# A decoder layer's expert stage: sums, norm and output unit by unit, in place of a last pass

## The chip, the cores and the metric

One core of one Trainium2 chip runs the whole kernel. The metric is device time of one launch in microseconds (us), lower is better; the median of three runs stands for the kernel.

## The reference

One decoder layer on x of 1024 tokens by 1024 (f32): a token mixer, a cross-attention, then the part that matters here, a mixture of experts with a residual and a layer norm. `h` is the second norm's output, `alpha = 2 ** 0.25`.

```python
h = layer_norm(alpha * h + memory_cross_attention(...), ln_x_g, ln_x_b)
p_g = softmax(h @ w_rg + b_rg); g = argmax(p_g)                     # one of 4 groups
e_val, e_idx = top_k((h @ w_re[g] + b_re[g]), 2)                    # two of its 8 experts
gate = p_g[g] * softmax(e_val)
y = sum(gate[c] * (silu(h @ w_gate[e]) * (h @ w_up[e])) @ w_down[e] for c, e in enumerate(e_idx))
out = layer_norm(alpha * h + y, ln_ffn_g, ln_ffn_b)
```

So each token has two experts, of one group, and 2048 (token, expert) rows are to be computed. An expert's weights are 12 tiles of 512 KB (8 for gate and up, 4 for down); 32 experts have 384.

## The kernel before

Up to about 840 us of the span come the mixer, the cross-attention, its norm and the router, tile by tile (8 tiles of 128 tokens). In the last loop over tiles (`for t in range(NT)`, L1101) PE's order is written out by hand; the other engines' order comes from a scheduler. `norm_pre`, `norm_stats` and `norm_post` make h2 (written to `h2_d` in DRAM), `route_a` finds the experts, `gates_` the gates, `route_b` each row's place within its expert; these run one tile behind the products of the next tile. Loads of the experts' weights into `ring` tiles are issued in this loop from SP: 35 tiles, and 42 with those added at L1190 and L1191.

After the loop, PE's and DVE's order is by hand (L1129). The last tile is normed and routed, then the lists are made. A **unit** is 32 rows of one expert; an expert has as many units as it needs, at least one, and the router's choice decides how many there are in all (78 here). `ohu` and `ohr` are one-hot matrices; their 16 f32 products (L1166) put, for each of 96 units and 32 places, the number of the row into `pi_`; from it come `gidx` (which quarter rows of h2 to gather) and `yidx` (where to write the result in `y_d`).

Then the experts' stage (`tile_critical`, L1368) runs with one program for each engine and semaphores by hand. A unit lies as 128 partitions x 256: 4 quarters of a row by 32 rows.

- SP loads weights into the ring, in the order in which experts run (expert 0 of each group, then expert 1 of each, ...). A load waits until the last unit of the expert that used its slot has done its `up` or `down` product.
- POOL gathers each unit's rows of h2 by an indirect DMA into `xg` (`get`, 8 ahead) and writes results by another (`put`).
- PE does `up` (64 products) and `down` (32 products). An expert's first `up` comes first, then for each further unit `up`, `down`, and then the last `down`.
- DVE turns `xg` (`rows`), multiplies by silu's result, turns again for `down`. ACT does silu and copies `down`'s result out of PSUM into `ys` (L1287).

Then comes the last pass (L1374 to L1395): for each tile, h2 and both results of each token are loaded, added with the gates, normed and written to `out`.

## Time and profile before

| | us |
|---|---|
| median of 3 runs | 1468.98 (1468.28 to 1471.16) |
| the profiled execution's own time | 1469.68 |
| its span, first to last instruction | 1467.9 |
| PE busy in the span | 1269.6 (86%) |
| DVE busy | 646.6 (44%) |
| ACT busy | 384.4 (26%) |
| POOL busy | 263.2 (18%) |

The span is what the rows below divide up; the profiled execution took 1.8 us more than its span. Busy times overlap between engines, so they don't add up to it.

### The profile page before, as it was taken

What the parts mean: (1) busy time and instruction counts of PE and PEld (TensorE: products, weight loads), DVE (VectorE), ACT (ScalarE), POOL (GpSimd) and SP (SyncE); (2) the same over time, 40 slices, a digit from 0 to 9 for tenths busy, and PEclk for the clock granted to TensorE, in tenths of its full rate; (3) what the DMA queues carried; (4) which work ended last, traced back from release to release, by engine and by line L of the source; (5) the groups of instructions that cost most, each with busy time, mean ns of one, the idle gap of its engine ahead of it and who ended that gap; (6) DMA issues with size and microseconds to landing.
All of it is one profiled execution on the core that took longest, in us unless ns stands there. A gap on an engine that the chain in (4) does not pass through costs nothing.

```text
span 1467.9 us, 29380 instructions
## 1 busy us (share of the span) xinstructions
PE 1269.6 (86%) x12171; PEld 979.3 (67%) x12171; DVE 646.6 (44%) x1585; ACT 384.4 (26%) x897; POOL 263.2 (18%) x301
## 2 busy tenths in 40 slices
PE   7999989999999999999999948988989869888700
PEld 6788866666677888888888737766657625647500
DVE  6676465555666558236577741111111111111148
ACT  4344354454664114225321101110101000001000
POOL 1111000000000221000011123333233322323303
PEclk9999999999999999999999959999999997999955
DMA  7003110101347322213632678999999999999583
GB/s 232 1 8 101 45 44 26 55 22 40 107 128 280 115 72 87 58 36 99 231 126 102 221 278 318 386 387 405 406 406 405 404 407 407 403 407 403 199 349 138
DMA packets 87789, 306.15 MB, mean 209 GB/s; under 512 B 12968, under 2 KB 13192, under 8 KB 87664
## 3 DMA queue, kind: packets, MB, share of 16 engines
q1 hardware_dynamic: 71424, 259.03, 46.5%
q0 software_dynamic: 13504, 35.43, 6.9%
q10 hardware_dynamic: 2736, 9.96, 1.7%
q8 instruction: 86, 1.41, 0.4%
q14 instruction: 39, 0.32, 0.1%
HBM read 282.04 MB, written 27.03 MB: 211 GB/s over the span
## 4 chain that ended last, share of the span: by engine, by line
PE 72%; SPq 8%; DMA 7%; DVE 7%; issue 3%; ACT 2%; POOLq 0%; POOL 0%; ACTq 0%; DVEq 0%
PE pg L1255 14%; SPq L1366 8%; PE py__7925 L1265 7%; DMA ring<-in_wx_dram 5%; PE py L101 4%; PE py L102 4%; PE py L103 4%; PE avf L641 3%; PE S L599 2%; PE ptf L627 2%; PE Sx L101 2%; PE Sx L103 2%; PE Sx L102 2%; PE S L598 2%; PE pk L101 2%
## 5 line engine op out<-in xcount | busy, mean ns | idle before, releaser
L1255 PE MATMUL pg<-ring,mo 128*32 128x256 f32 x4992 | 310.3, 392 | 45.8 <-DVE mo L1307 24.6
L1255 PEld LDWEIGHTS pg<-ring,mo 128*32 128x32 f32 x4992 | 209.0, 112 | 134.8 <-DVE mo L1307 39.5
L1307 DVE STREAM_TRANSPOSE mo<-xg 128x256 f32<-128x256 f32 x79 | 35.2, 445 | 382.8 <-PE pg L1255 374.3
L1265 PE MATMUL py__7925<-ring,mo 128*32 128x256 f32 x2496 | 160.0, 385 | 38.4 <-DVE mo L1316 22.0
L1265 PEld LDWEIGHTS py__7925<-ring,mo 128*32 128x32 f32 x2496 | 108.9, 110 | 76.7 <-DVE mo L1316 32.9
L1327 POOL DMA_INDIRECT xg<-h_d,gidx x86 | 87.8, 1021 | 300.2 <-ACT ys L1287 178.0
L1293 ACT ACTIVATE mo<-pg 128x128 f32<-128x128 f32 x78 | 21.7, 278 | 390.1 <-PE pg L1255 390.1
L1334 POOL DMA_INDIRECT y_d<-ys,yidx x78 | 79.1, 1015 | 80.5 <-ACT ys L1287 65.3
L604 DVE CUSTOM_DVE_ANT_0 S<-S,cB 128x128 f32<-128x128 f32 (+7 forms) x64 | 49.0, 765 | 62.2 <-PE S L602 59.8
L1316 DVE STREAM_TRANSPOSE mo<-mo 128x128 f32<-128x128 f32 x78 | 24.3, 311 | 67.4 <-PE py__7925 L1265 64.1
L101 PE MATMUL py<-B,Pxh 128*128 128x512 f32 x128 | 53.3, 416 | 0.0
L608 ACT ACTIVATE Pf<-S,fm 128x128 f32<-128x128 f32 (+7 forms) x64 | 47.3, 740 | 20.3 <-DVE fl L614 11.9
L1287 ACT ACTIVATE ys<-py__7925 128x256 f32<-128x256 f32 x78 | 29.8, 382 | 85.0 <-PE py__7925 L1265 82.1
L103 PE MATMUL py<-B,Pxl 128*128 128x512 f32 x128 | 50.2, 393 | 0.0
L101 PE MATMUL py<-woh,oh 128*128 128x512 f32 x128 | 50.1, 392 | 0.0
L102 PE MATMUL py<-B,Pxh 128*128 128x512 f32 x128 | 50.1, 392 | 0.0
L102 PE MATMUL py<-wol,oh 128*128 128x512 f32 x128 | 50.0, 391 | 0.0
L103 PE MATMUL py<-woh,ol 128*128 128x512 f32 x128 | 50.0, 391 | 0.0
L103 PE MATMUL Sx<-Ah,h1l 128*128 128x512 f32 x128 | 49.8, 389 | 0.0
L101 PE MATMUL Sx<-Ah,h1h 128*128 128x512 f32 x128 | 49.8, 389 | 0.0
L102 PE MATMUL Sx<-Al,h1h 128*128 128x512 f32 x128 | 49.8, 389 | 0.0
L627 PE MATMUL ptf<-identF,Pf 128*128 128x128 f32 x288 | 43.2, 276 | 2.4 <-DVE Pf L615 2.4
(502 smaller groups left out, 2684.5 us busy)
## 6 DMA issues: line engine op xcount, KB each, us to landing
ring<-in_wx_dram SPq DMA_DIRECT2D x384, 512.0 KB, 7.8
yb<-y_d SPq DMA_DIRECT2D x16, 512.0 KB, 8.8
h_d<-h POOLq DMA_DIRECT2D x15, 512.0 KB, 3.0
wqkr<-in_wqk_dram SPq DMA_DIRECT2D x8, 512.0 KB, 3.7
cB<-c_d POOLq DMA_DIRECT2D x8, 512.0 KB, 4.1
wkr<-in_wxkv_dram SPq DMA_DIRECT2D x8, 512.0 KB, 4.8
wor<-in_w_out_dram SPq DMA_DIRECT2D x8, 512.0 KB, 3.7
wxqr<-in_wxqT_dram SPq DMA_DIRECT2D x8, 512.0 KB, 3.7
```

The costliest lines, as they stand in the source:

```text
L101: mm(o, ah, bh, start=st, stop=False, skip_group_check=True)
L102: mm(o, ah, bl, start=False, stop=False, skip_group_check=True)
L103: mm(o, al, bh, start=False, stop=sp, skip_group_check=True)
L604: nc.vector.tensor_tensor_reduce(S[:, 0:n], S[:, 0:n], CB[h][:, 0:n], scale=1.0, scalar=3.0e38, op0=OP.add, op1=OP.min, accum_out=m_)
L608: nc.scalar.activation(p_[:, 0:n], S[:, 0:n], AF.Exp, bias=m_, scale=-1.0, accum_out=l_)
L627: nc.tensor.transpose(pt[:, j], p_[:, (4 * a + j) * P:(4 * a + j + 1) * P], identF)
L641: mm(av[64 * h:64 * h + 64, q0:256], V[p // 2, j // 4][:, j % 4, c0:c0 + 64], PT[i2, h, j // 4][:, j % 4, q0:256], start=j == 0, stop=j == ...
L1255: i_ = mm(pg[32 * h:32 * h + 32], xT_[:, k], w_[:, :, h * P:h * P + P], start=k == 0, stop=k == ND - 1, skip_group_check=True)
L1265: i_ = mm(py_[32 * h:32 * h + 32], aT[:, c], w_[:, h * 256:h * 256 + 256], start=c == 0, stop=c == 3, skip_group_check=True)
L1327: e.indirect_dma_start(out=xg[v % NG], out_offset=None, in_=h2v, in_offset=bass.IndirectOffsetOnAxis(ap=gidx[:, v:v + 1], axis=0), bounds_ ...
L1334: e.indirect_dma_start(out=yv, out_offset=bass.IndirectOffsetOnAxis(ap=yidx[:, j:j + 1], axis=0), in_=ys[j % NY], in_offset=None, bounds_c ...
L1366: e.dma_start(ring[n % NRING], wx[ordr[s], k]).then_inc(s_w[n % NRING], 16)
```

## The change

In the experts' stage a unit's result is no longer written away to be summed later. Experts run in rising order within a group, so the lower-numbered expert of a token runs first. For a row of a token's **first** expert, the unit holds gate * result + h2 (h2 is what `xg` still holds), and this sum is written, unnormed, to the token's row of `out`. For a row of the **second** expert, `xg` is gathered a second time, now from `out` (`again`: rows of first experts have an index out of bounds and are left as they are); gate * result is added to it, the norm is applied, and the row of `out` is written again.

The norm needs sums over a row's four quarters, which lie on four partitions: `bn_stats` of each quarter goes into `qst`, a product with `same` on PE (`moments`) brings the four together, `bn_aggr` merges them; the power runs on POOL (`root`). `sec` and `fst` (1 or 0 for each row of a unit) choose between the normed and the plain sum. A unit's `moments` comes two `up`s after its own `up`, and its `down` now comes after the next `up`, over the border between experts too. `put` of a unit comes two steps behind; `again` of a unit waits for the landing of the write four units earlier. `y_d`, `yidx`, `ys` and the last pass are gone; `out` is filled with zeros once, in the router's loop.

The lists are made from bf16 one-hots: `ohA` holds 256 (t + 1) at a row's place, `ohB` (made on ACT) the rest of its number in units of that, so that two bf16 products give the whole number; 32 products in place of 16 f32 ones, and the 16 `ohu` instructions become two `eq`. Further products (`pgt`, `pgc`) bring the gates to the units' rows, as three bf16 parts. After the last loop the routing of the last tile comes ahead of the second half of its norm, its gates come last, and the first gather is issued ahead of the stage. One tile less is added to the ring (41).

In the router's loop and the lists:

```diff
-    ohr = [s4("ohr", (P, 4, 2, P)) for _ in range(2)]
+    ohA, ohB = s4("ohA", (P, NT, 2, P), BF16), s4("ohB", (P, NT, 2, P), BF16)
+    ohG = s4("ohG", (P, NT, 2, 96), BF16)
+    z_ = s4("z_")
+    nc.gpsimd.memset(z_, 0.0)
+    for t in range(NT):
+        nc.gpsimd.dma_start(out[t * P:t * P + P, :], z_)
...
-        nc.vector.tensor_tensor(ohr[t // 4][:, t % 4], io4[:, None, :].to_broadcast([P, 2, P]),
-                                rf[:, :, None].to_broadcast([P, 2, P]), op=OP.is_equal)
+        for c in range(2):
+            nc.vector.tensor_scalar(ohA[:, t, c], io4, rf[:, c:c + 1], 2.0 * P * (t + 1),
+                                    op0=OP.is_equal, op1=OP.mult)
+        for c in range(2):
+            nc.scalar.activation(ohB[:, t, c], ohA[:, t, c], AF.Copy, scale=lo[:, c:c + 1])
...
-    norm_post(NT - 1)
+    norm_mid(NT - 1)
     route_a(NT - 1, logits(NT - 1))
-    route_b(NT - 1)
-    gates_(NT - 1)
+    pr = ranks(NT - 1)
...
+    norm_post(NT - 1, mid=False)
...
-            nc.vector.tensor_scalar(ohu, io96, unit[:, t, c:c + 1], dst1[:, t, c:c + 1],
-                                    op0=OP.is_equal, op1=OP.mult)
-            mm(pi_, ohr[t // 4][:, t % 4, c], ohu, start=t + c == 0, stop=t + c == NT)
+    for h in (slice(0, NT), slice(NT, 2 * NT)):
+        nc.vector.tensor_tensor(eq[:, h], io96[:, None, :].to_broadcast([P, NT, 96]),
+                                unit.rearrange("p t (c o) -> p (t c) o", o=1)[:, h].to_broadcast([P, NT, 96]),
+                                op=OP.is_equal)
+        for n in range(h.start, h.stop):
+            for o_ in (ohA, ohB):
+                mm(pi_, o_[:, n // 2, n % 2], eq[:, n], start=n == 0 and o_ is ohA, stop=n == 2 * NT - 1 and o_ is ohB)
...
+    EARLY = 1
+    for v in range(EARLY):
+        gather(xg[v], h2v, gidx[:, v:v + 1])
...
+    for v_, src in ((g3q, g3), (b3q, b3)):
+        for q in range(4):
+            nc.gpsimd.dma_start(v_[32 * q:32 * q + 32], bass.AP(tensor=src.tensor, offset=src.offset + 256 * q,
+                                                                ap=[[0, 32], [1, 256]]))
...
+    gates_(NT - 1)
+    gate_rows(NT - 1)
...
-    ring_tiles(SLOTS - 4 - PRE[-1], s4p, "s4", load=False)
+    ring_tiles(SLOTS - 5 - PRE[-1], s4p, "s4", load=False)
```

`gate_rows`, new and also called for each tile in the loop, is nine small DVE instructions (three bf16 parts of the gates, and their product with a one-hot of the place). PE's and ACT's programs in the experts' stage:

```diff
+        def moments():
+            e.wait_ge(s_ms, r)
+            mm(pst.rearrange("p q n -> p (q n)"), same, qst.rearrange("p q n -> p (q n)"),
+               start=True, stop=True).then_inc(s_st, 1)
...
             up(s)
+            if s:
+                moments()
+                down(s - 1)
...
                     up(s)
+                    moments()
                     down(s)
...
-            down(s)
+        moments()
+        down(NEXP - 1)
+        e.reg_add(r, r, 1)
+        moments()
...
-            e.activation(ys[j % NY], py_, AF.Copy).then_inc(s_ev, 1)
+            e.activation(w1, vs[j % NV], AF.Copy, scale=fst[:, j:j + 1]).then_inc(s_w1, 1)
```

DVE's (its waits are left out; `total(j)` waits for `down` of unit j, for the second gather of j and for the landing of the write of unit j - 4):

```diff
+        def total(j):
...
+            e.scalar_tensor_tensor(v, py_, gcol[:, j:j + 1], xg[j % NG], op0=OP.mult, op1=OP.add).then_inc(s_ev, 1)
...
+            e.bn_stats(st, v).then_inc(s_bn, 1)
...
+            e.tensor_tensor(qst, st[:, None, :].to_broadcast([P, 4, 6]),
+                            qm[:, :, None].to_broadcast([P, 4, 6]), op=OP.mult).then_inc(s_ms, 1)
+        def norm_a(j):
...
+            e.bn_aggr(mv, pst.rearrange("p q n -> p (q n)")).then_inc(s_ag, 1)
...
+            e.scalar_tensor_tensor(w1, b3q, sec[:, j:j + 1], w1, op0=OP.mult, op1=OP.add).then_inc(s_w2, 1)
...
+            e.tensor_scalar(rs[:, 0:1], mv[:, 1:2], EPS / ALPHA ** 2, None, op0=OP.add).then_inc(s_r1, 1)
+            e.scalar_tensor_tensor(v, v, mv[:, 0:1], g3q, op0=OP.subtract, op1=OP.mult).then_inc(s_nm, 1)
+        def norm_b(j):
...
+            e.tensor_tensor(rs[:, 1:2], rs[:, 1:2], sec[:, j:j + 1], op=OP.mult).then_inc(s_r3, 1)
...
+            e.scalar_tensor_tensor(v, v, rs[:, 1:2], w1, op0=OP.mult, op1=OP.add).then_inc(s_o, 1)
         def step(i):
             if i + 1 < UMAX:
                 rows(i + 1)
             w8(e, s_si, i + 1)
             e.tensor_mul(a_[i % 2], a_[i % 2], pg[:, 1]).then_inc(s_mu, 1)
+            if i > 1:
+                norm_a(i - 2)
             w8(e, s_mu, B_MU + i + 1)
             w8(e, s_dn, i)
             e.transpose(mo[:, 512:640], a_[i % 2]).then_inc(s_at, 1)
+            if i > 1:
+                norm_b(i - 2)
+            if i:
+                total(i - 1)
```

and POOL's (`LA` is 6):

```diff
+        def again(v):
+            if v < UMAX:
+                w8(e, s_xt, v + 1)
+                if v > 3:
+                    w8(e, s_y[(v - 4) % NV], 16 * ((v - 4) // NV + 1))
+                gather(xg[v % NG], outv, aidx[:, v:v + 1]).then_inc(s_g[v % NG], 16)
...
         def step(i):
-            get(i + NG)
-            if i:
-                put(i - 1)
+            if i > 1:
+                root(i - 2)
+            get(i + LA)
+            if i > 1:
+                put(i - 2)
+            again(i + 1)
```

## Rows read from the trace of the kernel before

**Rows 1.** The second part of the page: in 40 equal slices of the span (36.7 us each) the busy share of the DMA engines in tenths and what they moved.

```profile
DMA  7003110101347322213632678999999999999583
GB/s 232 1 8 101 45 44 26 55 22 40 107 128 280 115 72 87 58 36 99 231 126 102 221 278 318 386 387 405 406 406 405 404 407 407 403 407 403 199 349 138
```

**Rows 2.** Busy time by stretch (us of the span; busy us and count of instructions on PE, PEld, DVE, ACT, POOL; granted clock as a share of 2.4 GHz; DMA share; GB/s): one tile and its neighbour of the router's loop, the hand-over to the experts' stage, its middle, its end, the last pass.

```profile
815.00:830.00 15.00, 15.00 (x87) 12.66 (x86) 11.09 (x39) 2.88 (x7) 2.32 (x3) 1.00 0.39 120
878.00:888.00 10.00, 9.12 (x172) 6.70 (x176) 2.01 (x7) 1.17 (x4) 3.02 (x3) 1.00 0.13 40
900.00:1000.00 100.00, 89.69 (x1600) 71.22 (x1592) 15.55 (x50) 10.22 (x33) 33.36 (x33) 1.00 1.00 391
1370.00:1376.00 6.00, 6.00 (x118) 5.37 (x112) 0.93 (x3) 0.66 (x2) 2.64 (x3) 1.00 0.66 262
1412.00:1468.00 56.00, 0.00 (x0) 0.00 (x0) 49.05 (x56) 0.00 (x0) 16.42 (x16) 0.50 0.57 232
```

**Rows 3.** The chain that ended last, in order of time, from the last wait for weights to the end (start us, us, what).

```profile
1344.38 16.56 DMA ring<-in_wx_dram
...
1385.79 2.44 PE py__7925 L1265 x32
1388.70 0.74 issue
1389.45 2.36 DMA y_d<-ys,yidx
1392.35 5.55 POOLq L1368
...
1462.41 1.29 DVE hx L719
```

**Rows 4.** DMA traffic of the middle of the experts' stage, 890 to 1350 us (queue, kind: packets, MB, share of 16 engines). q1 carries the weights, q0 the indirect gathers and writes.

```profile
DMA packets 53237, 185.06 MB, mean 402 GB/s; under 512 B 8133, under 2 KB 8169, under 8 KB 53184
...
q1 hardware_dynamic: 46560, 169.54, 92.7%
q0 software_dynamic: 6624, 14.73, 8.7%
```

**Rows 5.** Groups of instructions of the experts' stage, 863 to 1392 us (line engine op out<-in shapes xcount | busy us, mean ns of one | idle time of the engine just before them, and what ended it).

```profile
L1265 PE MATMUL py__7925<-ring,mo 128*32 128x256 f32 x2496 | 160.0, 385 | 38.4 <-DVE mo L1316 22.0 <-issue 14.7 <-ACT ys L1287 1.1
...
L1327 POOL DMA_INDIRECT xg<-h_d,gidx x86 | 87.8, 1021 | 300.2 <-ACT ys L1287 178.0 <-PE pg L1255 91.9 <-issue 30.2
L1334 POOL DMA_INDIRECT y_d<-ys,yidx x78 | 79.1, 1015 | 80.5 <-ACT ys L1287 65.3 <-issue 15.2
L1307 DVE STREAM_TRANSPOSE mo<-xg 128x256 f32<-128x256 f32 x79 | 35.2, 445 | 382.8 <-PE pg L1255 374.3 <-DMA xg<-h_d,gidx 8.5
```

**Rows 6.** Timeline of the last pass: the half-row statistics of one tile and their merging on DVE, and the power on POOL for a tile in the middle and for a late one (start us, us, engine line op; in brackets the idle time before it and what ended it).

```profile
1415.86 1.29 DVE L1388 BATCH_NORM_STATS2 st<-hx 128x6 f32<-128x512 f32 x2
...
1418.29 0.20 DVE L1390 BATCH_NORM_AGGREGATE mv<-st 128x2 f32<-128x12 f32 x1
...
1426.56 1.46 POOL L1393 TENSOR_TENSOR rs<-rs,nhalf 128x1 f32<-128x1 f32 x1
...
1457.04 0.57 POOL L1393 TENSOR_TENSOR rs<-rs,nhalf 128x1 f32<-128x1 f32 x1
```

**Rows 7.** Timeline of the end of the norm, the lists and the entry into the experts' stage (start us, us, engine line op): the last part of the last tile's norm, one bf16 product of the ranks, the issue of that tile's write, the f32 products of the lists, the list of gathers, the last DVE instruction ahead of the stage, the first gather, the first transpose and the first unit.

```profile
842.84 1.41 DVE L1095 SCALAR_TENSOR_TENSOR h<-h,rs,b2v 128x512 f32<-128x512 f32 x2 [0.46 <-POOL rs L1086]
...
846.69 0.21 PE L1017 MATMUL pr<-M,low 128*128 128x32 bf16 x1 [4.25 <-DVE M L996]
...
848.75 0.35 ACTq L1096 DMA_DIRECT2D h_d<-h  x1
...
853.51 6.94 PE L1166 MATMUL pi__7845<-ohu,ohr 128*128 128x96 f32 x32 [2.07 <-DVE ohu L1164]
...
861.56 0.27 DVE L1175 TENSOR_SCALAR gidx<-scr,pcol 128x96 int32<-128x96 int32 x1
...
862.33 0.18 DVE L1182 TENSOR_TENSOR more<-more,cum 1x31 int32<-1x31 int32 x1
...
864.38 1.18 POOL L1327 DMA_INDIRECT xg<-h_d,gidx  x1 [21.58 <-issue]
...
871.06 0.45 DVE L1307 STREAM_TRANSPOSE mo<-xg 128x256 f32<-128x256 f32 x1 [8.55 <-DMA xg<-h_d,gidx]
...
871.56 6.40 PE L1255 MATMUL pg<-ring,mo 128*32 128x256 f32 x64 [11.11 <-DVE mo L1307]
```

**Rows 8.** Timeline of units of 32 rows (start us, us, engine line op; in brackets the idle time before it and what ended it): the third one of the first expert, a gather and a write issued back to back, and two downs in a row.

```profile
884.05 3.66 PE L1255 MATMUL pg<-ring,mo 128*32 128x256 f32 x64
...
896.54 1.03 POOL L1327 DMA_INDIRECT xg<-h_d,gidx  x1 [4.50 <-ACT ys L1287]
897.88 1.01 POOL L1334 DMA_INDIRECT y_d<-ys,yidx  x1 [0.30 <-issue]
...
907.78 2.00 PE L1265 MATMUL py__7925<-ring,mo 128*32 128x256 f32 x32
...
912.96 2.00 PE L1265 MATMUL py__7925<-ring,mo 128*32 128x256 f32 x32
```

**Rows 9.** DMA issues of the whole span by line (out<-in engine op xcount, KB each, median us from issue to landing): the write of the last tile of h2.

```profile
h_d<-h ACTq DMA_DIRECT2D x1, 512.0 KB, 8.2
```

More of the change, by code (lines that the diff above doesn't have):

```diff
@@ L1117, in layer @@
                 if (n, k) == (1, 2) and t > 0:
-                    route_b(t - 1)
+                    route_b(t - 1, ranks(t - 1))
+                    gate_rows(t - 1)
                 if (n, k) == (1, 3):
@@ new lines, in layer @@
+    d_i = ohs[:, 704:800].bitcast(I32)
+    gidx = consts.tile([P, 96], I32, name="gidx")
+    nc.vector.tensor_copy(d_i, pi_)
+    nc.vector.tensor_scalar(gidx, d_i, 1, None, op0=OP.logical_shift_right)
+    nc.vector.tensor_scalar(gidx, gidx, 4.0, pcol[:, 3:4], op0=OP.mult, op1=OP.add)
+    nc.vector.tensor_scalar(gidx, gidx, BIG - 1, None, op0=OP.bitwise_and)
+    xg2 = [s4("xg", (P, 4, 256)) for _ in range(2)]
+    xg = [xg2[n // 4][:, n % 4] for n in range(NG)]
+    for x_ in xg2:
+        nc.gpsimd.memset(x_, 0.0)
@@ L1182, in layer @@
     nc.vector.tensor_tensor(more[:, 1:32], more[:, 1:32], cum[:, 0:31], op=OP.subtract)
+    col = s4("col")
+    g3q, b3q = col[:, 0:256], col[:, 256:512]
+    for v_, src in ((g3q, g3), (b3q, b3)):
+        for q in range(4):
+            nc.gpsimd.dma_start(v_[32 * q:32 * q + 32], bass.AP(tensor=src.tensor, offset=src.offset + 256 * q,
+                                                                ap=[[0, 32], [1, 256]]))
+    sec, fst, gcol = col[:, 512:608], col[:, 608:704], col[:, 704:800]
+    aidx = col[:, 800:896].bitcast(I32)
+    nc.vector.tensor_scalar(d_i, d_i, 1, None, op0=OP.bitwise_and)
+    nc.vector.tensor_copy(sec, d_i)
+    nc.vector.tensor_scalar(fst, sec, -1.0, 1.0, op0=OP.mult, op1=OP.add)
+    nc.vector.scalar_tensor_tensor(aidx, fst, float(BIG), gidx, op0=OP.mult, op1=OP.add)
+    gates_(NT - 1)
+    gate_rows(NT - 1)
+    pgt = pw1("pgt", (96, 96))
+    for n in range(2 * NT):
+        mm(pgt, ohG[:, n // 2, n % 2], eq[:, n], start=n == 0, stop=n == 2 * NT - 1)
+    gpt = sm.tile([96, 96], F32, name="gpt")
+    nc.vector.tensor_copy(gpt, pgt)
+    pgc = pw1("pgc", (P, 96))
+    mm(pgc, same[0:96], gpt, start=True, stop=True)
+    nc.vector.tensor_copy(gcol, pgc)
     tail.close()
@@ L1199, in layer @@
     aT = mo[:, 512:640].rearrange("p (k r) -> p k r", r=32)
-    NY = 4
-    y4 = s4("ys", (P, NY, 256))
-    ys = [y4[:, n] for n in range(NY)]
+    w1 = mo[:, 640:896]
+    st, mv, rs = mo[:, 896:902], mo[:, 902:904], mo[:, 904:906]
+    vs4 = s4("vs", (P, NV, 256))
+    vs = [vs4[:, n] for n in range(NV)]
     pg = psm.tile([P, 2, P], F32, name="pg")
     py_ = psm.tile([P, 256], F32, name="py_")
-    h2v = h2_d.rearrange("t (q c) -> (t q) c", q=4)
-    yv = y_d.rearrange("t (q c) -> (t q) c", q=4)
+    pst = psm.tile([P, 4, 6], F32, name="pst")
     sem = lambda n: tc.alloc_semaphore(n)
-    s_up, s_dn, s_si, s_mu, s_at, s_xt, s_ev = (
-        sem(n) for n in ("up", "down", "silu", "mul", "flip", "rows", "out"))
+    s_up, s_dn, s_si, s_mu, s_at, s_xt, s_ev, s_bn, s_ms, s_st, s_ag, s_r1, s_r2, s_r3, s_nm, s_w1, s_w2, s_o = (
+        sem(n) for n in ("up", "down", "silu", "mul", "flip", "rows", "sum", "bn", "parts", "stats", "aggr", "var", "pow", "mask",
+                         "norm", "first", "bias", "done"))
     s_w = [sem(f"w{n}") for n in range(NRING)]
     s_g = [sem(f"g{n}") for n in range(NG)]
-    s_y = [sem(f"y{n}") for n in range(NY)]
-    B_MU, B_AT, B_EV = 1, 1, 2
+    s_y = [sem(f"y{n}") for n in range(NV)]
+    B_MU, B_AT, B_EV, B_MS = 1, 1, 2, 2
     def w8(eng, s, v):
@@ L1294, in step @@
             if i:
-                out_(i - 1)
-        units(e, step, lambda n: out_(n - 1))
+                first(i - 1)
+        units(e, step, lambda n: first(n - 1))
     def dve():
@@ L1316, in step, with end @@
             e.transpose(mo[:, 512:640], a_[i % 2]).then_inc(s_at, 1)
+            if i > 1:
+                norm_b(i - 2)
+            if i:
+                total(i - 1)
+        def end(n):
+            norm_a(n - 2)
+            norm_b(n - 2)
+            total(n - 1)
+            norm_a(n - 1)
+            norm_b(n - 1)
         rows(0)
-        units(e, step, lambda n: None)
+        units(e, step, end)
     def pool():
```

193 lines of the change are left out of this document (110 added, 83 removed).

## The prediction

> **What bounds the kernel now.** I read the page's slices first [rows 1]: from slice 24 to slice 36 the DMA engines stand at 9 and move some 405 GB/s, then come three slices of less. The stretches say why [rows 2]: in the middle of the experts' stage the DMA share is 1.00 while PE is busy 89.7 of 100 us, DVE 15.6 and POOL 33.4, so the loads of weights set the pace there; in the last pass (1412 to 1468) DVE is busy 49 of 56 us and PE not at all. The chain of waits [rows 3] joins the two: a last wait for weights ends at 1360.9 (1344.38 + 16.56), PE works off the last experts until 1388.2, the last write takes 2.36, the close of the stage 5.55, so the last pass begins at 1397.9 and its last DVE instruction ends at 1463.7. The traffic [rows 4] gives the price of bytes: 185.06 MB in 460 us, of which the gathers and writes (q0) are 14.73 MB. The stage has 78 units [rows 5]; from the first product at 871.6 [rows 7] to 1388.2 that is 6.6 us for a unit, while PE by itself does one in 5.18 (from one `down` to the next, [rows 8]).
>
> **The last pass goes.** From 1397.9 to the span's end at 1467.9 are 70.0 us. The close of the stage stays. Between the last DVE instruction and the span's end lie 4.2 us, a write and the program's own close; I keep 2 of them, an estimate with 0 and 4.2 as ends. Gain 68.0 (65.8 to 70). Behind the last `down` stood a copy and a wake of POOL, 1.2 us in all (1388.2 to 1389.45, [rows 3]). Now a chain stands there: the sum, the mask and three passes over 256 columns on DVE. Two statistics over 512 columns take 1.29 [rows 6], two passes over 512 columns 1.41 [rows 7], so 256 columns cost about 0.36: five such, 1.8. Merging takes 0.20, the power 0.57 [rows 6], the mask and two small ones about 0.2 each, the product of `moments` 0.3, and eight hand-overs some 0.1 each. That is about 4.3, less 0.4 for the pass that runs beside the power: 3.9, then the wake of 0.74 that was there before [rows 3]. Against 1.2 that is **+3.4** (2.5 to 6). The net of both: **-64.6**.
>
> **The second gather.** Its rows are 1024, one for each token, 4 KB each: 4.19 MB more on engines that are full. By q0's own time, 8.7% of 460 us for 14.73 MB, 40.0 us of all engines, this costs **+11.4**; by bytes alone at 402 GB/s it is 10.4; if every indirect DMA costs the same, valid rows or not (460 us hold 70 units with two each, so 40.0 over 140, 0.29 each), 78 of them cost 23. I take 11.4, since half of the rows are out of bounds; ends 0 (if the engines had room after all) and 23. The ring has 41 tiles in place of 42, so one load of 0.52 MB falls behind the start: **+1.3**. The writes are as many as before; `g3` and `b3` are 0.26 MB ahead of the stage and count nothing. The zeros are 4.2 MB, 10.4 us of full engines, in a loop where the DMA share is 0.39 and PE is never idle (15.00 of 15, [rows 2]): hidden; if a load of `hr` came late behind them, up to +10.
>
> **The engines within a unit.** All of these stand beside loads that give a unit 6.6 us, and 6.8 with the second gather. PE: `moments` is two passes of an f32 product; the lists' products take 0.217 a pass (6.94 over 32, [rows 7]) right after an idle stretch, at the full clock of the stage [rows 2] less, so 0.22 to 0.43; I take 0.25, a unit is 5.43. In exchange `down` comes after the next expert's `up`, and its waits for DVE's turn (22.0 us, and part of 14.7 of issue, [rows 5]) are covered. Neither shows while weights set the pace, but the waits are what keeps PE at 90%, so I count them as slack. DVE: 1.0 us a unit now (15.6 in 100 us), and about 2.6 more (5 x 0.36, 0.2 merging, three small ones); 3.6, with hand-overs 4.5, under 6.8. Behind DVE's `total`, which waits for the second gather, stand the turn of the next unit's rows and so PE's next `up`. POOL: three indirect DMAs of 1.02 with 0.30 between them [rows 5, 8] are 4.0, the power 0.57 to 1.46 [rows 6], one wake 0.74 [rows 3]: 5.3 to 6.2. Under 6.8, but it is the nearest. Behind POOL's waits for the norm and for the write's landing stand the gathers of later units, six ahead, which have room. ACT has a pass of the same size for the copy. All **0**; without the cover of the weights the step would be POOL's 5.3 to 6.2 a unit.
>
> The Trainium skill (SBUF — State Buffer, section "SBUF: two separate sides") says that VectorE with two SBUF inputs and a GpSimd instruction that reads SBUF lock each other out for a whole instruction. The trace agrees as far as it goes: the same power takes 1.46 beside DVE's long passes and 0.57 beside little [rows 6]; by that rule the power always costs POOL the 1.46, which is what the rival (B) below takes.
>
> **The lists and the start.** Off the chain go the gates' round over ACT (about 1.9), the wait of 0.46 for the power [rows 7] and two of six index instructions (0.5). The 32 bf16 products: one entry takes 0.21 [rows 7], so 6.7 us end to end, or half where loads of weights hide behind products; I take 3.5, half of them beside the second `eq`, whose price is 1.0 by 768 columns. From 853.1 to 860.4 become 4.0. So `gidx`, ready at 861.8, is ready near 856. But the gather needs the last tile's write of h2. It follows the norm's second half, now behind the ranks and `nu`, near 849.3 in place of 848.75, and took 8.2 to land [rows 9]: 857.5. The gather then lands 2.4 to 6.65 after its issue [rows 3, 7], 861 to 865. Meanwhile DVE has the index work of the second gather, the gates, `gate_rows` and two copies, about 6 us: until 862.3, where DVE ended before too (862.5, [rows 7]). POOL has eight small loads, at most 1.02 each if they come last: up to 867. So the first turn comes between 863.5 and 868.5 in place of 871.06: **-5** (-7.5 to -2.5; 0 if the write lands later). The first expert's three units take as long as before, and the ring is released, and the engines fill, as much earlier: until then they idle (share 0.13 from 878 to 888, [rows 2]; its third `up` ends at 887.7, [rows 8]).
>
> **The loop and the end.** A tile's DVE work was 11.1 of 15 us [rows 2]; the new one-hots and `gate_rows` add about 1.9, under PE's cover, though one more long-lived buffer leaves fewer for loads: **+1** (0 to 10). At the stage's end PE runs alone for some 27 us, since the loads thin out after 1370 (share 0.66, [rows 2]); six `moments` there: **+1.5**.
>
> **Sum.** -64.6 + 11.4 + 1.3 - 5 + 1 + 1.5 = -54.4. On the profiled span of 1467.9 this gives 1413.5, with the 1.8 around it 1415.3; the median of the runs lies 0.7 under that execution, so 1414.6.
>
> **Rivals.** (A) The second gather is hidden, because `down`'s new place takes PE's stalls out and the stage's start moves by the full 7.5. For it: PE idles 38.4 us ahead of `down` [rows 5]. Against it: a share of 1.00 has no room. 1414.6 - 11.4 - 2.5 = 1401. (B) POOL becomes the bound: if two of its four instructions pay the wake of 0.74 and the power its 1.46, a step is 4.0 + 1.46 + 1.5 = 6.9, with a little waiting 7.0. Then `up`s run from 866 for 78 x 7.0 and 4 for the cold first unit to 1416, against 1397 in my sum (1388.2 + 9.2): 1434. For it: in the kernel before `put` mostly waits, 65.3 of 80.5 idle us [rows 5]. Against it: back to back they need 0.30. (C) The time doesn't fall. `again` waits for the write four units earlier, which closes a ring: the write lands (up to 6.65), wake 0.74, gather lands (6.65), then sum, statistics, power and norm over two steps, about 11: 25 us for four units. Weights allow 4 x 6.8 = 27, so it decides from there; with landings of 9 in place of 6.65 it is 30, or 7.5 a unit: 78 x 7.5 from 866, 1455, and 58 over my sum: 1473. For it: three indirect DMAs a unit, not two, on full engines. Against it: 6.65 was measured beside the seven loads that fill the ring (42 less 35 tiles).
>
> The Trainium skill (DMA: Bandwidth & Descriptors, section "Anatomy of one DMA — SWDGE (gpsimd) path") prices a DMA of POOL's at 2.0 us plus bytes at 436 GB/s, an estimated 2.2 for these. The quiet write agrees (2.36, [rows 3]), the one beside loads does not (6.65, [rows 7]); by the page's price the ring would be 16 us and (C) impossible.
>
> **Chances and range.** My forecast 0.63, with a range of its own of 1404 to 1425 from the ends of the start, the second gather and the loop; (A) 0.12; (B) 0.19; (C) 0.06. A difference of 0.2%, 3 us, is what can be told from none. All but (C) are faster: 0.94; (C) reaches from no change, 0.02, to slower, 0.04. The range takes in most of (A) and (B): 1398 to 1447.
>
> **What would show it.** In the changed profile: no stretch without PE at the end, and some 15 us from the last `down` to the end of the span; a DMA share of 1.0 from about 882 to 1383; q0 with half as many packets again; the first `up` near 866; waits of PE for the ring's loads as before, and none for the turn ahead of `down`. POOL near 5.5 us a unit and mostly waiting for DVE would confirm its term. Wrong: PE waiting on `moments` or on the turn of `rows`, with DVE waiting for `xg` or for the power behind it, and the DMA share under 0.95 in the middle, would mean (B) or (C); the first `up` after 871 that the lists gained nothing.

## The result, and the profile after

The changed kernel takes **1428.84 us** (median of 4 runs, 1425.89 to 1429.52) against 1468.63 before (4 runs): ratio 0.972, interval 0.970 to 0.974. The forecast was 1414.6, so the direction is right and the time lies 14.2 above it. The profiled execution has a span of 1426.9 in place of 1467.9, 41.0 less.

The two kernels' traces can be cut at the same five places. "Loop" is from the first to the last start of the first operation of the router's norm on DVE, "start" from there to the first `up` of the experts' stage, "weights" to the end of the last wait for weights in the chain, "run" from there to the start of the last product of the last `down`, "closing" to the span's end. The table gives the changed kernel three times, profiled in three groups of runs, and the experiments that are told below, all in us.

| kernel | until the loop | loop | start | weights | run | closing | span |
|---|---|---|---|---|---|---|---|
| before | 730.3 | 109.0 | 32.3 | 489.3 | 26.4 | 80.6 | 1467.9 |
| changed | 733.5 | 116.5 | 24.5 | 504.4 | 32.0 | 16.0 | 1426.9 |
| changed, second profile | 730.5 | 117.6 | 24.0 | 503.9 | 32.5 | 15.3 | 1423.7 |
| changed, third profile | 729.1 | 116.6 | 24.1 | 503.7 | 33.1 | 15.9 | 1422.5 |
| zeros early | 733.8 | 109.0 | 26.0 | 503.3 | 32.7 | 16.6 | 1421.4 |
| second gather empty | 729.8 | 117.0 | 24.5 | 494.0 | 29.5 | 16.3 | 1411.1 |
| no second gather | 732.5 | 117.0 | 24.4 | 489.7 | 31.1 | 17.8 | 1412.5 |
| before, bf16 lists alone | 729.8 | 108.8 | 29.3 | 488.4 | 25.9 | 81.0 | 1463.2 |
| moments twice | 732.3 | 116.5 | 24.7 | 505.7 | 34.3 | 16.2 | 1429.7 |
| last down first | 729.7 | 117.0 | 24.0 | 505.2 | 31.2 | 16.9 | 1424.0 |
| three edits together | 731.1 | 108.9 | 25.9 | 504.5 | 30.6 | 17.4 | 1418.4 |
| late first gather | 732.9 | 116.9 | 30.6 | 502.5 | 32.5 | 16.1 | 1431.5 |

The first column scatters from 729.1 to 733.8 over kernels whose code up to there is that of the changed kernel or nearly so; the 3.2 us by which the changed kernel's first profile comes late there is scatter, not the change.

The page's slices of the changed kernel, which answer to [rows 1] (35.7 us each here): busy share of the DMA engines in tenths, and GB/s.

```profile
DMA  7002111101145523101473367999999999999991
GB/s 238 1 8 71 58 45 48 52 23 42 55 141 178 204 87 119 60 30 59 142 300 119 108 247 259 388 392 402 401 401 404 402 399 405 401 401 402 398 392 47
```

The engines stand at 9 up to the last slice but one; the three lighter slices of before are gone. Busy time by stretch in the changed kernel, which answers to [rows 2] (us; busy us and count on PE, PEld, DVE, ACT, POOL; granted clock; DMA share; GB/s):

```profile
878.00:888.00 10.00, 9.10 (x154) 5.56 (x150) 2.22 (x7) 0.56 (x2) 6.87 (x7) 0.95 0.74 278
900.00:1000.00 100.00, 97.58 (x1678) 57.89 (x1682) 57.28 (x202) 13.27 (x34) 63.88 (x68) 1.00 1.02 396
1370.00:1376.00 6.00, 3.02 (x35) 0.67 (x32) 0.59 (x2) 0.49 (x1) 2.04 (x2) 0.83 1.02 392
1378.90:1411.30 32.40, 30.16 (x468) 16.58 (x468) 17.11 (x60) 3.93 (x10) 19.16 (x20) 0.92 0.50 190
1411.30:1426.90 15.60, 0.62 (x2) 0.50 (x2) 4.41 (x15) 0.51 (x1) 3.52 (x4) 0.62 0.04 14
```

In the middle (900 to 1000) the DMA share is 1.02, as before, but PE is busy 97.6 of 100 us in place of 89.7, DVE 57 in place of 16, POOL 64 in place of 33. At 1370 the engines are still full, where before they had thinned out. The chain that ended last, which answers to [rows 3] (start us, us, what):

```profile
1361.10 17.82 DMA ring<-in_wx_dram
...
1408.99 0.41 PE pst L1363 x2
1409.40 2.33 issue
...
1415.06 0.64 PE pst L1363 x2
...
1418.73 1.03 POOL out_dram L1491
```

The last wait for weights ends at 1378.9 (1361.10 + 17.82), the last `down` works until 1411.3, and 15.6 us later the span is over; in the kernel before it was 80.2 (1387.7 to 1467.9). Traffic from 890 to 1350, which answers to [rows 4] (packets, MB, share of 16 engines):

```profile
DMA packets 54784, 183.10 MB, mean 398 GB/s; under 512 B 9643, under 2 KB 10031, under 8 KB 54723
...
q1 hardware_dynamic: 45211, 164.65, 90.8%
q0 software_dynamic: 9512, 17.59, 10.5%
```

q0 grew from 14.73 to 17.59 MB and from 6624 to 9512 packets; q1 brought 4.89 MB of weights less in the same 460 us. Groups of the stage, which answer to [rows 5] (busy us, mean ns | idle just before, and what ended it):

```profile
L1357 PE MATMUL py__8124<-ring,mo 128*32 128x256 f32 x2496 | 161.2, 401 | 0.0
L1240 POOL DMA_INDIRECT xg<-h_d,gidx x84 | 88.8, 1058 | 32.0 <-issue 22.1 <-DVE gp L1076 9.9
L1240 POOL DMA_INDIRECT xg<-out_dram,col x79 | 80.9, 1024 | 39.9 <-issue 25.9 <-DMA out_dram<-vs,gidx 8.4 <-DVE mo L1413 5.5
L1491 POOL DMA_INDIRECT out_dram<-vs,gidx x78 | 79.4, 1018 | 63.1 <-issue 33.7 <-DVE vs L1446 19.4 <-DMA out_dram<-vs,gidx 7.0
...
L1498 POOL TENSOR_TENSOR mo<-mo,nhalf 128x1 f32<-128x1 f32 x78 | 55.7, 714 | 120.6 <-DVE mo L1436 120.4
```

PE no longer idles ahead of `down` (0.0 in place of 38.4). POOL's power takes 0.714 on the mean and POOL waits 120 us for DVE ahead of it, so POOL isn't the bound. A unit costs POOL 1.06 + 1.02 + 1.02 + 0.71 and, by the idle of issue (22.1/84 + 25.9/79 + 33.7/78), 1.0 of its own time between them: 4.8.

### The profile page after: what moved, and what is told of

Same layout as the page of the kernel before. It is cut to its first block, busy times and chain, and to the rows that moved or that the text cites. A ratio compares the mean times of both kernels' runs of the same rounds, so it can differ in the third digit from the quotient of the medians.

```text
span 1426.9 us, 30910 instructions
## 1 busy us (share of the span) xinstructions
PE 1313.3 (92%) x12347; PEld 926.1 (65%) x12347; DVE 799.5 (56%) x2322; ACT 402.1 (28%) x913; POOL 394.9 (28%) x473
## 5 line engine op out<-in xcount | busy, mean ns | idle before, releaser
L1347 PE MATMUL pg<-ring,mo 128*32 128x256 f32 x4992 | 315.3, 399 | 50.6 <-DMA ring<-in_wx_dram 34.3
L1347 PEld LDWEIGHTS pg<-ring,mo 128*32 128x32 f32 x4992 | 163.0, 114 | 190.1 <-DMA ring<-in_wx_dram 59.4
L1392 ACT ACTIVATE mo<-vs,col 128x256 f32<-128x256 f32 x78 | 39.6, 508 | 275.8 <-DVE vs L1421 275.8
L1357 PEld LDWEIGHTS py__8124<-ring,mo 128*32 128x32 f32 x2496 | 75.8, 114 | 48.2 <-issue 8.5
L1240 POOL DMA_INDIRECT xg<-h_d,gidx x84 | 88.8, 1058 | 32.0 <-issue 22.1
L1491 POOL DMA_INDIRECT out_dram<-vs,gidx x78 | 79.4, 1018 | 63.1 <-issue 33.7
L1240 POOL DMA_INDIRECT xg<-out_dram,col x79 | 80.9, 1024 | 39.9 <-issue 25.9
L1498 POOL TENSOR_TENSOR mo<-mo,nhalf 128x1 f32<-128x1 f32 x78 | 55.7, 714 | 120.6 <-DVE mo L1436 120.4
L649 POOL DMA_DIRECT2D oT_d<-ofx x16 | 11.5, 718 | 183.1 <-ACT ofx L648 156.8
L1457 DVE STREAM_TRANSPOSE mo<-mo 128x128 f32<-128x128 f32 x78 | 24.4, 312 | 60.4 <-PE py__8124 L1357 60.4
L1363 PEld LDWEIGHTS pst<-qst,same 128*128 128x128 f32 x158 | 24.9, 199 | 41.8 <-issue 33.3
```

Of the source, the lines that this page charges most:

```text
L1240: return nc.gpsimd.indirect_dma_start(out=x_, out_offset=None, in_=src, in_offset=bass.IndirectOffsetOnAxis(ap=idx, axis=0), bounds_check= ...
L1347: i_ = mm(pg[32 * h:32 * h + 32], xT_[:, k], w_[:, :, h * P:h * P + P], start=k == 0, stop=k == ND - 1, skip_group_check=True)
L1357: i_ = mm(py_[32 * h:32 * h + 32], aT[:, c], w_[:, h * 256:h * 256 + 256], start=c == 0, stop=c == 3, skip_group_check=True)
L1392: e.activation(w1, vs[j % NV], AF.Copy, scale=fst[:, j:j + 1]).then_inc(s_w1, 1)
L1491: e.indirect_dma_start(out=outv, out_offset=bass.IndirectOffsetOnAxis(ap=gidx[:, j:j + 1], axis=0), in_=vs[j % NV], in_offset=None, bounds ...
L1498: e.tensor_tensor(rs[:, 1:2], rs[:, 0:1], nhalf, op=OP.pow).then_inc(s_r2, 1)
```

## Experiments

**The zeros.** In the changed kernel the loop is 7.5 us longer. Its timeline there (start us, us, engine line op; in brackets the idle time before and what ended it):

```profile
725.71 4.23 POOL L993 DMA_DIRECT2D out_dram<-z__6668  x8 [0.29 <-POOL i__6591 L936]
...
733.54 0.69 DVE L1133 SCALAR_TENSOR_TENSOR h<-hr,py 128x512 f32<-128x512 f32 x1 [0.90 <-PE py L105]
...
734.29 0.55 POOL L151 DMA_DIRECT2D g2v<-in_g_dram  x1 [4.08 <-DMA out_dram<-z__6668]
...
737.86 0.53 POOL L151 DMA_DIRECT2D b2v<-in_b_dram  x1 [3.03 <-DMA out_dram<-z__6668]
...
750.00 1.42 DVE L1150 SCALAR_TENSOR_TENSOR h<-h,mv,g2v 128x512 f32<-128x512 f32 x2 [7.97 <-DMA g2v<-in_g_dram]
...
754.75 0.68 DVE L1133 SCALAR_TENSOR_TENSOR h<-hr,py 128x512 f32<-128x512 f32 x1
```

POOL has issued its eight zero writes from 725.71 on, and the load of g2v (the norm's gain; b2v is its bias) waits 4.08 at its issue until the first of them has landed (734.0), that of b2v 3.03 until the second has (737.6). Once issued, the load of g2v takes 15.6 us to land, in place of 8.0 in the kernel before. DVE's first operation that needs g2v stands 7.97 us, and the next tile's norm begins behind it, at 754.75.

The DMA engines had little room there even before the change. The stretch in the kernel before, with the fields of [rows 2] (the last two are DMA share and GB/s):

```profile
720.00:740.00 20.00, 20.00 (x107) 17.00 (x107) 11.67 (x28) 4.85 (x9) 2.60 (x6) 1.00 0.87 327
```

and with the zeros, in the changed kernel:

```profile
725.00:750.00 25.00, 25.00 (x135) 21.11 (x133) 8.96 (x26) 4.46 (x8) 6.59 (x14) 1.00 1.00 389
```

So two things hold the load of g2v back: the writes ahead of it on POOL's queue, and engines that are full until 750. No run separates the two. The experiment writes the zeros at the kernel's start (its eight writes are issued from 7.2 to 16.2 us):

```diff
-    z_ = s4("z_")                       # in the router's loop
-    nc.gpsimd.memset(z_, 0.0)
-    for t in range(NT):
-        nc.gpsimd.dma_start(out[t * P:t * P + P, :], z_)
+    z_ = consts.tile([P, 256], F32, name="z_")      # ahead of the attention stage
+    nc.gpsimd.memset(z_, 0.0)
+    for t in range(NT):
+        nc.gpsimd.dma_start(out[...].rearrange("p (q c) -> p q c", q=4),
+                            z_[:, None, :].to_broadcast([P, 4, 256]))
```

> The changed kernel with its eight zero writes (4.2 MB) moved from the router's loop to the attention stage, where they are written from a small constant tile. Theory (they are no work that other work hides: on POOL's queue they stand ahead of the loads of g2v and b2v, and the second tile's norm waits for those loads, so the loop ends 7 to 8 us later): the time falls by 6 to 9 us, to 1420 to 1423, and the second tile's first norm_pre starts within 2 us of the kernel before (744.8). Rival (the later loop is the change's new work on DVE and ScalarE there, or the 4.2 MB as bytes wherever they are written): the time stays within 2 us of 1428.8.

Measured: 1422.61 (ratio 0.968, 0.965 to 0.970), 6.2 under the changed kernel. The first operation of the norm in the kernel before (count, ns, first and last start):

```profile
L1077 DVE SCALAR_TENSOR_TENSOR h<-hr,py x16: 676/686/689, 730.3 to 839.3; 128x512 f32<-128x512 f32 x16
```

in the changed kernel:

```profile
L1133 DVE SCALAR_TENSOR_TENSOR h<-hr,py x16: 676/683/690, 733.5 to 850.0; 128x512 f32<-128x512 f32 x16
```

and with the zeros early:

```profile
L1134 DVE SCALAR_TENSOR_TENSOR h<-hr,py x16: 675/686/689, 733.8 to 842.8; 128x512 f32<-128x512 f32 x16
```

From first to last 109.0, 116.5, and 109.0 again: the whole of the longer loop is the zeros, and the rest of the new work on DVE (one-hots, `gate_rows`) is hidden. Of the 7.5, 1.5 are lost again at the start, which is 26.0 there in place of 24.0 to 24.5: its first gather starts 2.6 behind the landing of h2's last write (860.8 to 863.4), where the changed kernel's starts 0.9 behind it (868.4 to 869.25). Why was not followed up, nor what the writes cost where they now stand (the loop is reached at 733.8, the latest of all, but within 0.3 of the changed kernel's first profile).

**The second gather.** Two kernels: one whose calls find every row number out of bounds, and one without the calls. Both leave out the first experts' part of the output.

```diff
-    nc.vector.scalar_tensor_tensor(aidx, fst, float(BIG), gidx, op0=OP.mult, op1=OP.add)
+    nc.vector.scalar_tensor_tensor(aidx, fst, 0.0, gidx, op0=OP.mult, op1=OP.add)
+    nc.vector.tensor_scalar(aidx, aidx, BIG, None, op0=OP.bitwise_or)
```
```diff
-                gather(xg[v % NG], outv, aidx[:, v:v + 1]).then_inc(s_g[v % NG], 16)
+                pass                    # and the waits for it in rows() and total() go
```

> The changed kernel with every row number of the second gather out of bounds: its 72 calls are still issued, but bring no rows; left out is the first expert's part in each second expert's row, so the output differs. Theory (the stage is bound by bytes, and the 4.2 MB of the second gather cost 10 to 12 us of the 15 by which the weights take longer): the time falls by 9 to 13 us, to 1416 to 1420, with the stretch from the first up to the last wait for weights at 492 to 495. Rival (the second gather moves under the weights' waits and the longer stretch is the units' longer chain on PE, DVE and POOL): no more than 3 us lower.

> The changed kernel without the second gather, calls and waits too (the output lacks the first expert's part, as in the run before this one). If the bytes are all that it costs, the time is that of the run with empty gathers, 1416 to 1420, within 2 us. If the calls themselves cost (POOL's time for 72 of them, or their descriptors in the queue), it is 3 us or more below that run.

Measured: 1415.52 (0.963, 0.961 to 0.966) and 1412.48 (0.960, 0.958 to 0.963). The weights stretch is 504.0 in the mean of the changed kernel's three profiles, 494.0 with empty calls and 489.7 without: 10.0 for the rows and 4.3 for calls without rows. Traffic from 890 to 1350 with empty calls:

```profile
DMA packets 56131, 184.11 MB, mean 400 GB/s; under 512 B 11280, under 2 KB 11316, under 8 KB 56069
...
q0 software_dynamic: 9792, 14.72, 9.1%
```

and without calls:

```profile
DMA packets 53137, 184.96 MB, mean 402 GB/s; under 512 B 8067, under 2 KB 8103, under 8 KB 53076
...
q0 software_dynamic: 6599, 14.82, 8.6%
```

The bytes are the same to 1% (14.72 and 14.82 MB for 69 or so units), but the empty calls make some 3200 packets under 512 bytes more, about 46 a call, and q0's share is 9.1% in place of 8.6. That these packets are the 4.3 us is a reading that fits; no run varied their number alone. In the changed kernel, where half of the rows exist, there are only some 1600 such packets more than without calls (9643 against 8067), so there the calls may cost less than 4.3 and the rows more than 10.0.

The split also depends on where the last wait for weights falls, since the run at the end is 2.5 to 3.6 shorter with empty calls. From the first `up` to the start of the last product (weights and run together) the three take 536.4, 523.5 and 520.8: 12.9 for the rows and 2.7 for empty calls. By the times alone the rows are clear and the calls are not: the intervals of the two kernels overlap. The rival (a longer chain of the units) is out: those two kernels keep the whole chain of sum, statistics and norm, and the one without calls has the weights stretch of the kernel before to 0.4 us (489.7 and 489.3). That 0.4 holds the ring's missing tile too.

**The moments.** A product more in each unit, or the last one moved:

```diff
-            mm(pst..., same, qst..., start=True, stop=True).then_inc(s_st, 1)
+            for _ in range(2):
+                i_ = mm(pst..., same, qst..., start=True, stop=True)
+            i_.then_inc(s_st, 1)
```
```diff
-        moments()
         down(NEXP - 1)
+        moments()
         e.reg_add(r, r, 1)
         moments()
```

> The changed kernel as it is, beside the three others of this group, so that small differences are read on one chip. Expected: 1426 to 1432, ratio 0.970 to 0.975 to the kernel before.

> The changed kernel with each unit's moments product issued twice (same numbers into the same place). Theory (where the loads of weights bound the stage, PE's extra 0.3 to 0.45 us of each unit only shortens its wait for weights; it counts in the six units after the last wait and in the last product): 1.5 to 4 us slower than the changed kernel, and the stretch from the first up to the last wait for weights at 504 as before it, within 1.5. Rival (the units' chain on PE sets the longer stretch): 77 times 0.3 to 0.45, 20 us or more slower.

> The changed kernel with the last down issued ahead of the moments product of the unit before it, which waits for DVE while down doesn't need it. Theory (PE stood 2.6 us idle there): 1.5 to 3 us faster than the changed kernel. Rival (the norm of the last-but-one unit comes later by as much as down comes earlier, and the closing takes it back): within 0.7 us of it.

Measured, in one group on one chip: the changed kernel 1428.50 (0.971, 0.969 to 0.973), moments twice 1428.92 (0.971, 0.969 to 0.973), last down first 1426.24 (0.970, 0.968 to 0.972). Doubling costs nothing that can be told by the times, less than the 1.5 to 4 of its theory and far from 20 us: by the profile PE's extra product lies under the weights (505.7 against 503.7 to 504.4), and the run at the end is longer (34.3 against 32.0 to 33.1). The moved `down` is inconclusive by the times (intervals overlap); by the profiles the run is 0.8 to 1.9 shorter and the closing 0.9 to 1.6 longer, as its rival said.

The end of the changed kernel in its timeline:

```profile
1393.62 1.93 PE L1357 MATMUL py__8124<-ring,mo 128*32 128x256 f32 x32
...
1399.27 1.93 PE L1357 MATMUL py__8124<-ring,mo 128*32 128x256 f32 x32
...
1408.99 0.40 PE L1363 MATMUL pst<-qst,same 128*128 128x24 f32 x2 [2.14 <-DVE qst L1425]
...
1409.32 1.93 PE L1357 MATMUL py__8124<-ring,mo 128*32 128x256 f32 x32
...
1411.74 0.27 DVE L1432 BATCH_NORM_AGGREGATE mo<-pst 128x2 f32<-128x24 f32 x1 [2.80 <-issue]
...
1413.85 0.48 DVE L1421 SCALAR_TENSOR_TENSOR vs<-py__8124,col,xg 128x256 f32<-128x256 f32 x1
```

Two `down`s in a row are 5.65 apart (5.18 before [rows 8]), and the last one stands behind a product of moments that waits 2.14 for `qst`. DVE's merge at 1411.74 comes after 2.80 us in which it waited for nothing that the profile shows; 2.33 of them are in the chain above. DVE then finishes the norm of the last unit but one, so its sum of the last unit starts at 1413.85, 2.6 after the end of the last `down`.

**The start.** The lists alone, put into the kernel before; then the changed kernel with its first gather late; then with the norm's old order.

```diff
-            nc.vector.tensor_scalar(ohu, io96, unit[:, t, c:c + 1], dst1[:, t, c:c + 1], ...)
-            mm(pi_, ohr[t // 4][:, t % 4, c], ohu, start=t + c == 0, stop=t + c == NT)
+            for o_ in (ohA, ohB):       # bf16, the number as a constant and a scale
+                mm(pi_, o_[:, n // 2, n % 2], eq[:, n], ...)
```
```diff
-    EARLY = 1
+    EARLY = 0
```
```diff
-    norm_mid(NT - 1)
+    norm_post(NT - 1)
     route_a(NT - 1, logits(NT - 1))
     ...
-    norm_post(NT - 1, mid=False)
```

> The kernel before with only the lists made by bf16 products (bf16 one-hots, the number split into a constant and a scale, 32 bf16 products in place of 16 f32 ones); the last pass, the norm's order and the units are as before. Theory (f32 products 6.9 us against 2.8, and two wide comparisons in place of sixteen; the rest of the earlier first unit comes from other moved steps): 3 to 6 us faster than before, 1463 to 1466, with the first up that much earlier. Rival (the gain at the start is due to the norm's order and the early first gather alone): within 1 us of before.

> The changed kernel with the first gather issued after the entry into the stage, with the other gathers, as the kernel before has it, and no longer from the list stage. Theory (of the 7.8 us by which the first up comes earlier after the last norm_pre, lists by bf16 alone gave 3.0; the early first gather is the larger part of the other 4.8): the stretch from the last norm_pre to the first up is 27 to 29 us in place of 24.0 to 24.7, and the time 2 to 4 us longer. Rival (the gather was waiting for h2's write anyway, and the norm's order made the 4.8): less than 1.5 us longer.

> The changed kernel with the last tile's norm finished ahead of its logits and route, as in the kernel before (all four operations on h2 and its write first). Two readings: the write of h2 then lands earlier but the route on DVE comes about 1.4 us later (two 128x512 operations); if the first gather is held by h2's landing (868.4, gather 869.3), the stretch from the last norm_pre to the first up stays within 1 us of 24.0 to 24.7 or shortens by it; if by the lists (index ready at 867.6), it is 1 to 2 us longer.

The lists alone: 1466.85 (0.998, 0.996 to 0.999), 3.2 less, and the start 29.3 in place of 32.3. The other two came out at 1449.41 and 1449.92, 21 us over the changed kernel, which neither reading foresaw. They had run on another chip than the kernels before, with the kernel before at 1469.81 as ever. So the first of them was run again beside the changed kernel:

> The changed kernel as it is, beside the one with the late first gather again. That one and the one with the norm first each took 1449 to 1450, and in both PE's instructions stood without a visible cause in the middle of the units (a down of 1.34 us from its first to its last load of weights took 2.2 to 2.8 in a third of them). Theory 1 (it belongs to the chip on which these two ran, not to the edits): here both kernels of this call are alike, both near 1449 or both near 1428. Theory 2 (the edits shift something in PE's supply of instructions): this kernel takes 1426 to 1432 and the other 1446 to 1452.

> As the run of this kernel before, on the same chip as the changed kernel of this call. Theory 1 (the chip): within 4 us of the changed kernel of this call, whichever level that has. Theory 2 (the edit): 1446 to 1452 with the changed kernel at 1426 to 1432.

Measured on that third chip: the changed kernel 1426.89 (0.972, 0.970 to 0.973), the late first gather 1433.27 (0.975, 0.973 to 0.977). Neither theory's numbers hold exactly, but the 1449 is gone with the same code, so it came with that chip or that occasion and not with the code; the edit itself costs 6.4 (more than the 2 to 4 of its theory), and its start is 30.6 in place of 24.1. DVE's waits there:

```profile
DVE mo L1413 <- DMA xg<-h_d,gidx: 8.0, 1, 8.0
```

The first transpose of rows stands 8.0 us for the first gather, which now is issued only inside the stage. The early first gather is thus worth 6.5 us, the lists 3.0, and all the rest of the change takes some 1.3 back (29.3 to 30.6); what of it does so was not separated. With the norm's old order the start is 24.9, within 1 us of 24.0 to 24.7, as the reading by h2's landing said. That run was on the chip of the 1449, but the start is not disturbed there: the late first gather has 30.4 on it and 30.6 on the third chip. So the norm's order gains little or nothing.

What the first gather waits for, in the changed kernel's timeline:

```profile
855.32 2.10 POOL L1258 DMA_DIRECT2D col<-in_g_dram  x4
857.41 1.96 POOL L1258 DMA_DIRECT2D col<-in_b_dram  x4
860.76 0.35 ACTq L1159 DMA_DIRECT2D h_d<-h  x1
869.25 1.14 POOL L1240 DMA_INDIRECT xg<-h_d,gidx  x1 [9.89 <-DVE gp L1076]
```

The write of h2's last tile, issued at 860.76, lands at 868.4, and the gather starts 0.9 later; in the other two profiles of this kernel it is 0.9 as well. The instruction in the bracket, a cast of the gates, is none that the gather needs. POOL's eight small loads were issued before that, and POOL then stood 9.89.

**What the chip with 1449 did.** Loads of PE's weights for one `moments` and one `down` of the late-gather kernel on that chip (start us, us, count; idle before):

```profile
1341.81 0.37 PEld L1363 LDWEIGHTS pst<-qst,same 128*128 128x128 f32 x2 [0.41 <-issue]
1342.22 0.14 PEld L1357 LDWEIGHTS py__8121<-ring,mo 128*32 128x32 f32 x3
1342.74 0.18 PEld L1357 LDWEIGHTS py__8121<-ring,mo 128*32 128x32 f32 x5 [0.38 <-issue]
1343.49 1.06 PEld L1357 LDWEIGHTS py__8121<-ring,mo 128*32 128x32 f32 x24 [0.57 <-issue]
```

and on the third chip, the same code:

```profile
1397.81 0.30 PEld L1363 LDWEIGHTS pst<-qst,same 128*128 128x128 f32 x2 [0.41 <-issue]
1398.14 1.45 PEld L1357 LDWEIGHTS py__8121<-ring,mo 128*32 128x32 f32 x32
```

Here 32 loads run in 1.45 us, there they stop after 3 and after 8 for 0.38 and 0.57 with nothing that the profile can name. Sums of the two groups over 890 to 1350 on that chip:

```profile
L1347 PEld LDWEIGHTS pg<-ring,mo 128*32 128x32 f32 x4160 | 175.0, 111 | 104.7 <-issue 43.3 <-DMA ring<-in_wx_dram 10.0 <-DVE mo L1413 4.8
L1357 PEld LDWEIGHTS py__8121<-ring,mo 128*32 128x32 f32 x2074 | 76.5, 109 | 56.8 <-issue 35.2
```

and on the third:

```profile
L1347 PEld LDWEIGHTS pg<-ring,mo 128*32 128x32 f32 x4288 | 137.6, 112 | 164.5 <-DMA ring<-in_wx_dram 56.8 <-issue 26.7
L1357 PEld LDWEIGHTS py__8121<-ring,mo 128*32 128x32 f32 x2168 | 65.7, 114 | 41.6 <-issue 6.9
```

The idle of issue is 78.5 us in place of 33.6, and PE hardly waits for weights any more (10.0 in place of 56.8). PE itself, with these stops, had become the bound: the chain's last wait for weights ends at 1249.0 there, and at 1382.9 on the third chip. The granted clock is no part of it, 0.974 on the mean there against 0.953. What makes the loads stop is open. The changed kernel was not run on that chip, so whether it stands at 1449 there too is open.

**Together.** Zeros early, last `down` first, and the last tile's `gates_` moved to where DVE waits for the lists' products:

```diff
+    gates_(NT - 1)
     d_i = ohs[:, 704:800].bitcast(I32)
     ...
-    gates_(NT - 1)
     gate_rows(NT - 1)
```

> The changed kernel with three edits: the zeros written early from a constant tile, the last down ahead of the moments before it, and the last tile's gates computed on DVE while it waits for the lists' products. Sum of the parts by the traces: zeros 6 to 7.5, the end 1.5 to 3, the gates up to 1.9 that come back only if the first gather is there by then (it landed at 872.2, the stage's entry came at 873.5, so 0 to 1.3): 8 to 11 us faster than the changed kernel, 1417 to 1421. If the parts don't add (the earlier start meets a ring of weights that is less full), 5 to 7.

Measured: 1420.15 (0.966, 0.964 to 0.968), 8.3 under the changed kernel in the same group. The table says from where: the loop is 8.7 shorter; of the run's 1.9 the closing takes 2.1 back; the gates bring nothing, the start is 25.9. This is the fastest complete version here, and it is in the main the early zeros.

## Why the prediction was right or wrong

Its sum was made for a span of 1413.5; the span is 1426.9, 13.4 more. The terms, in its order:

- **The last pass goes: right in size, in part by luck.** Forecast -64.6; the closing went from 80.6 to 16.0, -64.6. Two errors cancel in it. The operations behind the last `down` are those that were written out, but the last write is issued 7.5 after its end (1411.25 to 1418.73) where the working has 4.6: DVE stands until 1411.74 and first has the norm of the unit before to finish. From that issue to the span's end it is 8.2 where 10.4 had been counted, a write and a close of the stage as before and 2 for the program's own.
- **The second gather: right in kind, short in size.** Forecast +11.4, measured 14.3 in the weights stretch, 15.6 with the run. Rows cost 10.0 to 12.9 by the two ways of cutting, near the 10.4 of bytes alone; calls without any row cost 4.3 or 2.7. What was too small is the price, q0's mean share for each byte: it spreads the cost of a call over the bytes, while here half of the rows are not there and their calls are. The bound of 23 for calls that all cost alike is out.
- **One ring tile less: too high.** Forecast +1.3; in the weights stretch without the second gather the tile, the longer unit and all the rest come to 0.4 together.
- **The zeros: wrong, and the largest miss.** They were taken as hidden, with +1 for the loop's other work. The step read a DMA share of 0.39 and a busy PE as cover, but read them from 815 to 830. The zeros moved between 725 and 750, where the share had been 0.87 before them (720 to 740) and became 1.00; and it did not look at the queue, on which the loads of g2v and b2v stood behind the writes, and behind those loads the next tile's norm on DVE. The bound of up to 10 was there, but for `hr`, for which DVE did not wait. Measured +7.5 for the loop where +1 was taken.
- **The start: better than forecast.** -5 was taken, with -7.5 as the end; the start went from 32.3 to 24.0 to 24.5, -7.8 to -8.3. The gather did wait for the last tile's write: it landed at 868.4, 18.3 after the last first operation of the norm, where the working has 18.2 (839.3 to 857.5). What was too cautious was POOL's eight small loads, which don't delay the first turn: they were issued ahead of the first gather, from 855.3 to 859.4, while POOL waited for that landing anyway. One of its signs would have misled: the first `up` came at 874.5, after 871, though the lists gained 3.0, because the loop ended 10.7 later.
- **The end: too low.** +1.5 for six products of 0.25; measured +5.6 (26.4 to 32.0). A unit is 5.65 instead of 5.43, so six cost 2.8 against 5.18; and the last `moments` but one waits 2.14 on PE for the sum of its unit, with the last `down` queued behind. That wait was in the order of the code and was not read off it. The other 0.7 was not traced.
- **Engines within a unit: right.** DVE was put at 3.6 and is at 3.4 (57.28 us for the 17 units between 900 and 1000). POOL was put at 5.3 to 6.2 and takes 4.8. PE's waits for the turn ahead of `down` are gone and became slack, and the doubled moments cost nothing that can be told.

Sum of the deviations, forecast to measured: loop with the scatter ahead of it +9.7, start -2.8, second gather and ring +2.4, end +4.1, closing 0.0: the 13.4. The better start hides 2.8 of what the other terms missed.

Of the rivals, (A) is out: without the second gather the weights stretch is 14.3 shorter, so it isn't hidden. (C) is out: the time fell, and POOL's waits for a write's landing are 15.4 us in the whole stage (8.4 + 7.0). The estimate of 2.2 beside it should be 2.3 for 128 KB by its own price, which changes nothing. (B) is out as it was told, since POOL waits for DVE. What it warned of, a unit that outgrows the weights' 6.6, did occur on one chip, in the kernels that took 1449 (6.9 a unit near the end), but on PE.

By the Trainium skill (SBUF — State Buffer, section "SBUF: two separate sides"), of a VectorE instruction with two SBUF inputs and a GpSimd instruction that reads SBUF, the one that starts first holds the ports that they share for its whole length. The prediction took from it that every power costs 1.46; that price did not come, the power takes 0.714 on the mean here, between the two prices of the trace before. No run here isolates the rule itself, and nothing in the sum hung on it.

## What to carry to other kernels

Price an added write in the stretch in which it will move, and not by the share of another one: here 0.39 was read and 0.87 was there. And look at what is issued behind it on the same queue, a small load that somebody waits for above all. Where loads of weights set the pace, an added transfer costs about its bytes at the pace of the full engines (10.0 to 12.9 where bytes gave 10.4), and indirect calls whose rows don't exist seem to cost something too. A program's slack on the engine next to the bound is worth keeping: here a unit of 5.65 on PE under 6.5 for the weights was enough on two chips, and on another, where PE's weight loads stopped, the two kernels tried were PE-bound.

## What was not expected of the hardware

- The same code took 1449.41 on one chip and 1433.27 on another, while the kernel before, on the same two, took the same 1469.81. PE's loads of weights stop in the middle of a `down` on the first (0.38 and 0.57 us, with no releaser in the trace).
- An indirect gather without a single valid row still makes some 46 packets under 512 bytes. All 79 such calls together took 2.7 to 4.3 us of a stage that the DMA engines bound, by one profile each; that the packets are the cause was not tested.
- The write of h2's last tile, 0.5 MB, was issued at 860.8 and had landed at 868.4; in the changed kernel the first gather starts 0.9 behind this landing, and in the kernel with the norm's old order as well (867.4 to 868.3).
